# The first feed-forward product by Strassen's scheme, with weight sums made by adding DMAs, in a two-layer encoder on one core

## The chip, the cores and the metric

The kernel runs on one NeuronCore of a Trainium2 chip. TensorE (PE) multiplies, VectorE (DVE) and ScalarE (ACT) work element by element, GpSimd (POOL) and SyncE (SP) issue DMAs here. The metric is the device time of one execution in microseconds, as the median of several runs.

## What is computed

Two layers on x of 512 tokens by 1024 channels, in float32: an attention part with three groups of heads, an output projection, and a feed-forward part of width 4096. The change lies in the feed-forward part, and in small places of the attention.

```python
for i in range(DEPTH):                       # DEPTH = 2
    h = rmsnorm(x, norm_mix[i])
    qa, ka, va, qb, kb, vb, cq, ckv, kr = jnp.split(h @ w_in[i], split_at, axis=-1)
    ...                                      # 6 + 4 + 6 heads, QK norms, rotary keys, biases
    x = x + mixed @ w_out[i]                 # 1024 x 1024
    h = rmsnorm(x, norm_mlp[i])
    x = x + jnp.square(jax.nn.relu(h @ w_up[i])) @ w_down[i]   # 1024 x 4096, 4096 x 1024
```

## The kernel before

**Numbers.** Each float32 operand is split in a high part (`whi`, or the first of a pair of tiles) that PE's fast float32r format holds exactly, and the rest (`wlo`, or the second). `split` does it with a copy, on ACT or DVE, and a subtraction on DVE that reads the source again. `mm3` multiplies two such pairs with three matmuls: high by high, high by low, low by high. Weights come by DMA into `raw` (2 buffers, `wload`) and are split by `wsplit` into `whi` and `wlo` (4 buffers each, 1024 columns).

**Order.** Nothing is issued as the code is written. The class `Plan` records each operation with its tiles, then `schedule` goes through them with assumed costs and delays and places, at each step, the operation that can start first; among equals the one with the lower turn. A turn is the place in the code plus an offset from the table `TURNS`, one offset for eight operations. Buffers of a tag are given out in the order of the code, except for the PSUM banks. A copy that may run on ACT or DVE (`copy`) goes where it would end first. The result is one fixed order for each engine.

**Stages of a layer.** `mix` holds input projections, 16 heads (`attend`, for each head two halves of 256 queries; each half's output sums up in a bank of its own, and `pv_out` adds the two half sums of products that stand in the upper and lower 64 rows), and the output projection in three groups. When the last group of the output projection has ended for half of the channels, `norm_in` transposes x for the channel tiles k, scales and splits them: `xg2[k]`, 512 tokens wide.

**Feed-forward, `mlp`.** The 4096 hidden channels are taken in 4 chunks (`CH`) of 1024. In a chunk, 8 blocks f of 128 hidden channels are made: `w_up` for the block (512 KB) is loaded and split, 8 k times `mm3` with 512 tokens as columns go into one bank, ACT does relu out of the bank, DVE multiplies it with the bank's relu into `sp` (tag `p`). Two blocks that are added and subtracted by Strassen's second product share one `sp`: DVE forms the signed sums (`q0`, `q2`, `q13`), and the hidden pieces A11, A22, A12 and S1 to S4 are split into tiles of the tags tm12, tm9, ma, vb, tm6, o. The second product, `w_down`, goes by Strassen's scheme in Winograd's form: 7 products of half size instead of 8, x_ij with tokens in halves and output channels in halves. Its four weight quarters are loaded whole in 1 MB DMAs into the tag `qk`, and `total` makes four sums of weights on DVE (b1, b2, b3, and b2 again) into the tag `pt`, which `product` splits. `add` adds a finished bank, times the row scale, to x.

The lines read `L326` in the profile of the kernel before, since `emit` issues every operation from one line; so the rows are told apart by tile names.

## Time and profile before

| | us |
|---|---|
| median of 3 runs | 1211.63 (1210.93 to 1211.81) |
| profiled execution, device time | 1210.97 |
| its span, first to last instruction | 1209.0 |
| PE busy in the span | 1194.9 (99%) |
| DVE busy | 1008.5 (83%) |
| ACT busy | 638.9 (53%) |
| POOL busy | 3.5 |
| DMA, share of 16 engines | about a third, 123.9 MB moved |

An engine is busy while it works on an instruction; waiting for a semaphore isn't busy. Matmuls are pipelined, so their rows overlap: the distance between the starts of two is what one costs, not its own duration. Groups of instructions give the tiles written and read, the shape, the count, the busy time, the mean duration, and the idle time of the engine just before.

### The profile page before, as it was taken

How to read it: one execution, taken by the hardware profiler on the slowest of the kernel's cores; microseconds unless marked ns; L12 is line 12 of the kernel's file. 1: busy time of each engine (PE TensorE's matmuls, PEld its weight loads, DVE VectorE, ACT ScalarE, POOL GpSimd, SP SyncE). 2: the span in 40 equal slices, each digit the busy share in tenths (PEclk: the TensorE clock that was granted, in tenths of full speed). 3: DMA queues.
4: the chain of work that ended last, by engine and by line, in shares of the span. 5: the costliest groups of instructions: out<-in, count | busy, mean ns of one | idle time of the engine just before them, and what ended most of it. 6: DMA issues, size and time to landing. Idle time of an engine off the chain costs nothing.

```text
span 1209.0 us, 17753 instructions
## 1 busy us (share of the span) xinstructions
PE 1194.9 (99%) x6624; PEld 1028.3 (85%) x6624; DVE 1008.5 (83%) x1902; ACT 638.9 (53%) x1237; POOL 3.5 (0%) x10
## 2 busy tenths in 40 slices
PE   9999999999999999999999999999999999999998
PEld 8998998788888888888899999887888888888886
DVE  7898899996886887948958988899978869679586
ACT  6667789644423533425547576976643334343242
POOL 1000000000000000000000000000000000000000
PEclk9999999999999999999999999999999999999999
DMA  6221254542133142221142303356322431423301
GB/s 215 95 88 36 75 140 124 165 157 91 67 132 112 70 147 98 75 99 55 60 144 90 106 18 90 105 159 189 117 93 82 139 105 70 138 72 106 104 2 68
DMA packets 36357, 123.89 MB, mean 102 GB/s; under 512 B 4700, under 2 KB 5852, under 8 KB 32176
## 3 DMA queue, kind: packets, MB, share of 16 engines
q1 hardware_dynamic: 36048, 122.41, 31.6%
q8 instruction: 52, 0.85, 0.3%
q0 software_dynamic: 224, 0.36, 0.1%
q14 instruction: 33, 0.27, 0.1%
HBM read 108.29 MB, written 4.24 MB: 93 GB/s over the span
## 4 chain that ended last, share of the span: by engine, by line
PE 89%; ACT 4%; DVE 3%; DMA 1%; issue 1%; SPq 0%; ACTq 0%; DVEq 0%
PE bank L326 89%; ACT p L326 1%; ACT pt L326 1%; DMA qk<-qk 1%; ACT sq L326 0%; DMA v<-in_xT_dram 0%; DVE v L326 0%; ACT pvt L326 0%; DVE pt L326 0%; DVE qk L326 0%; DMA raw<-in_w_out_dram 0%; DVE o L326 0%; DVE p L326 0%; ACT tm L326 0%; DVE tm L326 0%
## 5 line engine op out<-in xcount | busy, mean ns | idle before, releaser
L326 PE MATMUL bank<-fm,whi 128*128 128x512 f32 x1024 | 315.0, 390 | 0.0
L326 PE MATMUL bank<-whi,fm 128*128 128x256 f32 (+2 forms) x1280 | 289.9, 311 | 1.7 <-ACT fm L326 0.8
L326 PEld LDWEIGHTS bank<-fm,whi 128*128 128x128 f32 x1024 | 192.1, 188 | 40.3
L326 PEld LDWEIGHTS bank<-whi,fm 128*128 128x128 f32 x1280 | 211.7, 190 | 13.6 <-ACT whi L326 1.0
L326 PE MATMUL bank<-wlo,fm 128*128 128x256 f32 (+2 forms) x640 | 196.4, 310 | 0.0
L326 PE MATMUL bank<-fm,wlo 128*128 128x512 f32 x512 | 196.3, 390 | 0.0
L326 ACT ACTIVATE whi<-raw 128x1024 fp32r<-128x1024 f32 (+2 forms) x102 | 105.0, 1032 | 168.5 <-PE bank L326 125.0
L326 DVE TENSOR_TENSOR wlo<-raw,whi 128x1024 fp32r<-128x1024 f32 (+2 forms) x122 | 142.2, 1170 | 60.1 <-ACT whi L326 59.5
L326 PE MATMUL bank<-whi,tm 128*128 128x512 f32 x544 | 178.4, 391 | 0.0
L326 PEld LDWEIGHTS bank<-wlo,fm 128*128 128x128 f32 x640 | 121.2, 190 | 5.3 <-DVE wlo L326 0.2
L326 ACT ACTIVATE whi<-pt 128x1024 fp32r<-128x1024 f32 x61 | 64.4, 1061 | 113.4 <-PE bank L326 80.3
L326 PEld LDWEIGHTS bank<-whi,tm 128*128 128x128 f32 x544 | 102.1, 188 | 22.4
L326 PE MATMUL bank<-wlo,tm 128*128 128x512 f32 x304 | 118.1, 391 | 0.0
L326 PEld LDWEIGHTS bank<-fm,wlo 128*128 128x128 f32 x512 | 96.1, 188 | 20.2
L326 PE MATMUL bank<-qk 96*128 96x512 f32 (+3 forms) x304 | 89.1, 395 | 1.4 <-DMA qk<-qk 0.5
L326 DVE TENSOR_TENSOR pt<-bank,pt 128x512 fp32r<-128x512 f32 (+2 forms) x128 | 79.5, 634 | 5.4 <-ACT pt L326 4.3
L326 DVE TENSOR_TENSOR wlo<-pt,whi 128x1024 fp32r<-128x1024 f32 x64 | 77.6, 1218 | 5.8 <-ACT whi L326 5.6
L326 ACT ACTIVATE whi<-qk 128x1024 fp32r<-128x1024 f32 x45 | 47.5, 1059 | 59.8 <-PE bank L326 59.8
L326 PE MATMUL bank<-con_sb,p 128*128 128x128 f32 x464 | 72.9, 275 | 2.8 <-DVE nm L326 1.0
L326 DVE TENSOR_TENSOR wlo<-qk,whi 128x1024 fp32r<-128x1024 f32 x48 | 58.3, 1219 | 19.4 <-ACT whi L326 19.4
L326 ACT ACTIVATE pt<-bank 128x512 fp32r<-128x512 f32 (+2 forms) x125 | 67.0, 552 | 2.3 <-PE bank L326 1.4
L326 PEld LDWEIGHTS bank<-wlo,tm 128*128 128x128 f32 x304 | 57.1, 188 | 12.7 <-DVE wlo L326 0.2
(186 smaller groups left out, 1887.0 us busy)
## 6 DMA issues: line engine op xcount, KB each, us to landing
qk<-in_w_down_dram SPq DMA_DIRECT2D x32, 1024.0 KB, 4.6
raw<-in_w_up_dram SPq DMA_DIRECT2D x64, 512.0 KB, 3.3
raw<-in_w_in_dram SPq DMA_DIRECT2D x28, 512.0 KB, 3.4
qk<-qk SPq DMA_DIRECT2D x78, 128.0 KB, 2.4
raw<-in_w_out_dram SPq DMA_DIRECT2D x16, 512.0 KB, 4.0
ma<-brow SPq DMA_DIRECT2D x12, 448.0 KB, 3.9
raw<-in_w_in_dram SPq DMA_DIRECT2D x8, 288.0 KB, 4.0
v<-in_xT_dram SPq DMA_DIRECT2D x6, 256.0 KB, 5.8
```

Source lines behind the costliest of these rows:

```text
L326: getattr(getattr(nc, o.eng), o.name)(*[real(a) for a in o.args], **{k: real(v) for k, v in o.kw.items()})
```

## The change

**First product.** h @ w_up also goes by Strassen's scheme. `seven` replaces `norm_in`: for two pairs of channel tiles at a time it brings x^T into one tile, splits A11, A22, A12 as they are and, after `combine` has formed the signed sums on DVE, S1 to S4. These tiles lie in the tags fm, qk and pt and stay for the whole layer. In a chunk the 1024 hidden channels are made in two pieces, `piece(0)` and `piece(1)`, each with 7 products of 2 x 4 `mm3` of 256 columns. The two run interleaved in the order of `UP`. The products that are summed share a bank; ACT takes intermediate sums out of the banks, DVE adds.

**Weight sums.** A weight tile `ta` (tag `qk`, two halves of 512 KB) is loaded with w11 and, after it has been split and used, `gps.dma_start(..., accum_op=OP.add)` adds w12, then w22, then w21 to it from DRAM: three versions follow the first, for the first product per piece, for the second product per half. The sum of w12 and w22 alone is made on DVE (in `raw`), since both are needed.

**Relu squared.** ACT does relu and then the square, from SBUF or from the bank, into `sp` (now tag `pt`, two hidden blocks side by side); `combine` forms the signed sums.

**Smaller.** A head's two halves sum up in the two halves of one bank, and `pv_out` runs once per head on 512 columns. `raw` has 3 buffers. The rotary tables lie in a tile `ma`. The running sum of squares (`Stat`) shares the tag `pvt`. `TURNS` is a new table. For adding DMAs `schedule` assumes another delay. `w_up` is laid out in the order in which the pieces read it.

```diff
--- before.py
+++ after.py
...
+UP = "00101100010111"
...
-            lat = self.LAT[e]
+            lat = 2500.0 + o.args[0].size() * 2.5 if e == "gpsimd" and o.name == "dma_start" else self.LAT[e]
...
+    def combine(v):
+        lead = (slice(None),) * (len(v.a.shape) - 1)
+        q0, q1, q2, q3 = (v[lead + (slice(i * 256, (i + 1) * 256),)] for i in range(4))
+        dve.tensor_tensor(q0, q1, q0, OP.subtract)
+        dve.scalar_tensor_tensor(q2, q0, -1.0, q2, OP.mult, OP.subtract)
+        dve.scalar_tensor_tensor(q1, q2, -1.0, q1, OP.mult, OP.subtract)
+        dve.scalar_tensor_tensor(q3, q2, -1.0, q3, OP.mult, OP.subtract)
+    def seven(supply, l, ks):
+        shared = supply(), supply()
+        raws, out = [], []
+        for n, k in enumerate(ks):
+            raw = T([128, 1024], F32, "p", 2)
+            for u in range(2):
+                pt = bank()
+                kk = k + 2 * u
+                for b in range(NB):
+                    pe.transpose(pt[:, b * 128:(b + 1) * 128], x_t[b][:, kk * 128:(kk + 1) * 128], ident)
+                copy(raw[:, u * 512:(u + 1) * 512], pt[:], P(l, G2 + kk))
+            r, sa, sb = ((supply(), supply()) for _ in range(3))
+            split(r[0], r[1], raw[:, 256:768])
+            half = slice(n * 256, (n + 1) * 256)
+            split(shared[0][:, half], shared[1][:, half], raw[:, 768:1024])
+            raws.append((raw, sa, sb))
+            lo, hi = slice(0, 256), slice(256, 512)
+            out.append({"a11": at(r, lo), "a22": at(r, hi), "a12": at(shared, half),
+                        "s3": at(sa, lo), "s1": at(sa, hi), "s2": at(sb, lo), "s4": at(sb, hi)})
+        for raw, sa, sb in raws:
+            combine(raw)
+            split(sa[0], sa[1], raw[:, 0:512])
+            split(sb[0], sb[1], raw[:, 512:1024])
+        return out
...
-        def pv_out(o, e, ps, cols):
+        def pv_out(o, e, ps):
             main, oth = slice(64 * e, 64 * e + 64), slice(64 - 64 * e, 128 - 64 * e)
-            n = cols.stop - cols.start
-            t = T([128, 256], F32, "pvt", 1)
-            copy(t[main, :n], ps[oth, :n])
-            dve.tensor_tensor(o[main, cols], ps[main, :n], t[main, :n], OP.add)
+            t = T([128, S], F32, "pvt", 1)
+            copy(t[main], ps[oth])
+            dve.tensor_tensor(o[main], ps[main], t[main], OP.add)
...
-                    xg2 += [norm_in(k, P(l, G2 + k)) for k in range(4 * h, 4 * h + 4)]
+                    xg2 += seven(lambda: next(supply), l, (4 * h, 4 * h + 1))
...
-            quarter = []
-            for q in range(4):
-                t = T([128, 2048], F32, "qk", QK)
-                dma.dma_start(t[:], w_down[l, :, (c * 4 + q) * 2048:(c * 4 + q + 1) * 2048])
-                quarter.append(t)
-            w11, w12, w21, w22 = quarter
+            def load(t, w):
+                for i in range(2):
+                    dma.dma_start(t[i], w[i])
+            def grow(t, w):
+                for i in range(2):
+                    gps.dma_start(t[i], w[i], accum_op=OP.add)
+            def pair(w, v, use, use2):
+                for i in range(2):
+                    a, b = (T([128, 1024], F32, "raw", 3) for _ in range(2))
+                    dma.dma_start(a[:], w[i])
+                    dma.dma_start(b[:], v[i])
+                    dve.tensor_tensor(a[:], a[:], b[:], OP.add)
+                    use(i, wsplit(a[:]))
+                    use2(i, wsplit(b[:]))
+            def blocks(w, o):
+                return [[w[l, :, o + q * 2048 + i * 1024:o + q * 2048 + (i + 1) * 1024] for i in range(2)] for q in range(4)]
+            w11, w12, w21, w22 = blocks(w_up, c * 8192)
...
-            for j in range(4):
-                sp = T([128, 1024], F32, "p", 2)
-                for u in range(2):
-                    f = c * 8 + u * 4 + j
-                    w = wload(w_up[l, :, f * 1024:(f + 1) * 1024])
-                    ps = bank()
-                    for k in range(KT):
-                        mm3(ps[:], at(w, slice(k * 128, k * 128 + 128)), (xg2[k][0][:], xg2[k][1][:]), k == 0, k == KT - 1)
-                    t = T([128, S], F32, "sq", 2)
-                    act.activation(t[:], ps[:], AF.Relu)
-                    dve.scalar_tensor_tensor(sp[:, u * 512:(u + 1) * 512], ps[:], 0.0, t[:], OP.max, OP.mult)
-                hr, lr, hs, ls = hid[j]
-                split(hr, lr, sp[:, 256:1024])
-                q0, q1, q2 = sp[:, 0:256], sp[:, 256:512], sp[:, 512:768]
-                q13 = sp[:].rearrange("p (x n) -> p x n", n=512)[:, :, 256:512]
-                dve.tensor_tensor(q0, q1, q0, OP.subtract)
-                dve.scalar_tensor_tensor(q2, q0, -1.0, q2, OP.mult, OP.subtract)
-                dve.scalar_tensor_tensor(q13, q2.unsqueeze(1).to_broadcast([128, 2, 256]), -1.0, q13, OP.mult, OP.subtract)
-                split(hs, ls, sp[:])
+            ta = chain()
+            load(ta, w11)
+            def square(t, dst, sign=1.0, src=None):
+                act.activation(t, t if src is None else src, AF.Relu, scale=sign)
+                act.activation(dst, t.rearrange("p (x n) -> p x n", x=2), AF.Square)
+            def piece(i):
+                def times(ps, key, hl, start):
+                    for n in range(2):
+                        for j in range(4):
+                            k = (n * 4 + j) * 128
+                            mm3(ps[:, n * 256:(n + 1) * 256], at(hl, slice(k, k + 128)), xg2[j][key],
+                                start and n == 0 and j == 0, n == 1 and j == 3)
+                w, more = ta[i], lambda v: gps.dma_start(ta[i], v[i], accum_op=OP.add)
+                px = bank()
+                times(px, "a11", wsplit(w), True)
+                e1 = T([128, S], F32, "sq", 2)
+                act.activation(e1[:], px[:], AF.Copy)
+                more(w12)
+                yield
+                py = bank()
+                times(py, "a12", wload(w21[i]), True)
+                dve.tensor_tensor(e1[:], py[:], e1[:], OP.add)
+                sp = T([128, 2, 1024], F32, "pt", 2)
+                square(e1[:], sp[:, :, 256:512])
+                yield
+                pz = bank()
+                times(pz, "s1", wsplit(w), True)
+                e2 = T([128, 1024], F32, "p", 2)
+                z, u = e2[:, :512], e2[:, 512:]
+                act.activation(z, pz[:], AF.Copy)
+                more(w22)
+                yield
+                times(px, "s2", wsplit(w), False)
+                act.activation(u, px[:], AF.Copy)
+                more(w21)
+                yield
+                r12, r22 = (T([128, 1024], F32, "raw", 3) for _ in range(2))
+                dma.dma_start(r12[:], w12[i])
+                dma.dma_start(r22[:], w22[i])
+                dve.tensor_tensor(r12[:], r12[:], r22[:], OP.add)
+                times(px, "s3", wsplit(r12[:]), False)
+                dve.tensor_tensor(z, px[:], z, OP.add)
+                square(z, sp[:, :, 512:768], -1.0)
+                yield
+                times(pz, "s4", wsplit(r22[:]), False)
+                dve.tensor_tensor(u, pz[:], u, OP.add)
+                square(u, sp[:, :, 768:1024], -1.0)
+                for n in range(2):
+                    split(hid[2 * i + n][0], hid[2 * i + n][1], sp[:, n, 256:1024])
+                yield
+                times(px, "a22", wsplit(w), False)
+                e4 = T([128, S], F32, "sq", 2)
+                square(e4[:], sp[:, :, 0:256], 1.0, px[:])
+                combine(sp)
+                for n in range(2):
+                    split(hid[2 * i + n][2], hid[2 * i + n][3], sp[:, n])
+                yield
+            both = piece(0), piece(1)
+            for i in UP:
+                next(both[int(i)])
...
+            def into(ps, a, start):
+                def use(i, hl):
                     for j in range(2):
                         for n in range(2):
                             mm3(ps[n][:], at(a[2 * i + j], slice(n * 128, (n + 1) * 128)), at(hl, slice(j * 512, (j + 1) * 512)),
                                 start and i == 0 and j == 0, i == 1 and j == 1)
+                return use
+            def product(ps, a, w, start):
+                for i in range(2):
+                    into(ps, a, start)(i, wsplit(w[i]) if isinstance(w[i], View) else wload(w[i]))
...
+            ta = chain()
+            load(ta, w11)
             ps_x = [bank(), bank()]
-            product(ps_x, a11, w11, True)
+            product(ps_x, a11, ta, True)
+            grow(ta, w12)
             add(ps_x, t1, c1, 1)
             ps_y = [bank(), bank()]
             product(ps_y, a12, w21, True)
             add(ps_y, t1, c1, 1, True)
-            b1 = T([128, 2048], F32, "pt", 2)
-            total(b1, w11, w12)
-            b2 = T([128, 2048], F32, "pt", 2)
-            total(b2, b1, w22)
-            product(ps_x, s2, b2, False)
+            ps_z = [bank(), bank()]
+            product(ps_z, s1, ta, True)
+            grow(ta, w22)
+            add(ps_z, t2, c2, -1)
+            product(ps_x, s2, ta, False)
+            grow(ta, w21)
             add(ps_x, t1, c2, -1)
-            ps_z = [bank(), bank()]
-            product(ps_z, s1, b1, True)
-            add(ps_z, t2, c2, -1)
-            b3 = T([128, 2048], F32, "pt", 2)
-            total(b3, w12, w22)
-            product(ps_x, s3, b3, False)
+            pair(w12, w22, into(ps_x, s3, False), into(ps_z, s4, False))
             add(ps_x, t2, c2, -1, True)
-            product(ps_z, s4, w22, False)
             add(ps_z, t1, c2, -1, True)
             if not last and c == CH - 1:
                 xg += [norm_in(k, P(l + 1, G1 + k)) for k in range(4)]
-            total(b2, b2, w21)
-            product(ps_x, a22, b2, False)
+            product(ps_x, a22, ta, False)
             add(ps_x, t2, c1, 1, True)
...
```

What stands where, before and after, on three engines. Numbers behind names tell buffers apart.

DVE, kernel before, layer 1, up stage of the second chunk: `p` is the hidden block `sp`, `wlo` the low part of a weight tile, `vb` holds hidden pieces.

```order
L326 SCALAR_TENSOR_TENSOR p_4573<-bank_4490,sq_4561 128x512
L326 TENSOR_TENSOR wlo_4580<-raw_4532,whi_4567 128x1024
L326 TENSOR_TENSOR p_4573<-p_4573 128x256
L326 CAST whi_4602<-raw_4576 128x1024
L326 SCALAR_TENSOR_TENSOR p_4573<-bank_4556,sq_4599 128x512
L326 TENSOR_TENSOR wlo_4610<-raw_4576,whi_4602 128x1024
L326 TENSOR_TENSOR vb_4614<-p_4573,vb_4614 128x768
L326 SCALAR_TENSOR_TENSOR p_4573<-p_4573 128x256
L326 SCALAR_TENSOR_TENSOR p_4573<-p_4573 128x2x256
```

DVE, kernel after, layer 1, start of the up stage of the third chunk. `qk_5045` is `ta` of that chunk; its first version is split in the first row (piece 0) and in `wlo_5455` (piece 1), the second versions in `wlo_5492` and `wlo_5540`, the third of piece 0 in `wlo_5579`.

```order
L333 TENSOR_TENSOR wlo_5398<-qk_5045,whi_5391 128x1024
L333 SCALAR_TENSOR_TENSOR v_3078<-bank_5155,r2p_4106,v_3078 128x512
L333 SCALAR_TENSOR_TENSOR v_3078<-bank_5145,r2m_4109,v_3078 128x512
L333 TENSOR_TENSOR wlo_5425<-raw_5298,whi_5413 128x1024
L333 TENSOR_TENSOR wlo_5455<-qk_5045,whi_5442 128x1024
L333 TENSOR_TENSOR sq_5452<-bank_5440,sq_5452 128x512
L333 TENSOR_TENSOR raw_5348<-raw_5348,raw_5438 128x1024
L333 TENSOR_TENSOR wlo_5492<-qk_5045,whi_5478 128x1024
L333 TENSOR_TENSOR wlo_5504<-raw_5339,whi_5497 128x1024
L333 SCALAR_TENSOR_TENSOR v_3078<-bank_5145,r2p_4106,v_3078 128x512
L333 TENSOR_TENSOR wlo_5540<-qk_5045,whi_5529 128x1024
L333 TENSOR_TENSOR wlo_5579<-qk_5045,whi_5568 128x1024
```

It goes on without a gap:

```order
L333 TENSOR_TENSOR wlo_5601<-raw_5348,whi_5587 128x1024
L333 CAST whi_5631<-qk_5045 128x1024
L333 TENSOR_TENSOR wlo_5639<-raw_5438,whi_5624 128x1024
L333 TENSOR_TENSOR wlo_5651<-qk_5045,whi_5631 128x1024
L333 TENSOR_TENSOR raw_5520<-raw_5520,raw_5614 128x1024
L333 TENSOR_TENSOR p_5543<-bank_5402,p_5543 128x512
L333 TENSOR_TENSOR wlo_5695<-qk_5045,whi_5666 128x1024
L333 TENSOR_TENSOR wlo_5711<-raw_5520,whi_5686 128x1024
L333 TENSOR_TENSOR sq_5704<-bank_5508,sq_5704 128x512
L333 CAST whi_5740<-raw_5614 128x1024
L333 TENSOR_TENSOR p_5543<-bank_5506,p_5543 128x512
L333 TENSOR_TENSOR wlo_5755<-raw_5614,whi_5740 128x1024
```

The row after these is `wlo_5768<-qk_5045,whi_5751`, the fourth version of piece 1. Relu-squares out of a bank are gone from DVE; subtractions for versions of `ta`, sums of weights in `raw`, and additions of `p` or `sq` stand in their place.

POOL, kernel before, all its DMAs: constants and the setup of the first layer.

```order
L326 DMA con_sb_67<-in_con_dram 128x272
L326 DMA tm9_148<-in_table_dram 32x10
L326 DMA tm6_165<-in_onehot_dram 32x1024
L326 DMA tm9_185<-in_nlogc_dram 10x1024
L326 DMA pi_199<-in_pos_dram 128x4
L326 DMA brow_308<-tm9_185 10x1024
```

POOL, kernel after, from the last DMA of the setup to the up stage of the fourth chunk of layer 1; the list goes on in the same way through layer 2.

```order
L333 DMA brow_297<-tm9_175 10x1024
L333 DMA qk_3547<-in_w_up_dram 128x1024 x6
L333 DMA qk_3497<-in_w_down_dram 128x1024 x6
L333 DMA qk_4298<-in_w_up_dram 128x1024 x6
L333 DMA qk_4625<-in_w_down_dram 128x1024 x6
L333 DMA qk_5045<-in_w_up_dram 128x1024 x6
L333 DMA qk_5387<-in_w_down_dram 128x1024 x6
L333 DMA qk_5792<-in_w_up_dram 128x1024 x6
```

Every row with x6 is six adding DMAs, one behind the other on this queue: three for each of two halves of `ta`. Each waits for the split of the version before.

PE, kernel before, up stage: `fm` are the parts of x^T, all 512 tokens wide.

```order
L326 MATMUL bank_5698<-fm_3868,whi_5687 128x512
L326 MATMUL bank_5698<-fm_3855,wlo_5695 128x512
L326 MATMUL bank_5698<-fm_3896,whi_5687 128x512
L326 MATMUL bank_5698<-fm_3916,whi_5687 128x512
L326 MATMUL bank_5698<-fm_3896,wlo_5695 128x512
```

PE, kernel after, the same place in a product of the third chunk: halves of `fm`, `qk` and `pt` tiles with the same weights.

```order
L333 MATMUL bank_5440<-fm_3776,whi_5413 128x256
L333 MATMUL bank_5440<-fm_3783,whi_5413 128x256
L333 MATMUL bank_5440<-fm_3776,wlo_5425 128x256
L333 MATMUL bank_5440<-fm_3776,whi_5413 128x256
L333 MATMUL bank_5440<-fm_3783,whi_5413 128x256
L333 MATMUL bank_5440<-fm_3776,wlo_5425 128x256
```

The pattern of three is the same, the width is 256.

## Rows read from the trace of the kernel before

**Rows 1.** The page: span; busy time, share of the span, instructions.

```profile
span 1209.0 us, 17753 instructions
PE 1194.9 (99%) x6624; PEld 1028.3 (85%) x6624; DVE 1008.5 (83%) x1902; ACT 638.9 (53%) x1237; POOL 3.5 (0%) x10
```

**Rows 2.** Windows by stage; columns in the first line.

```profile
core 0: us, PE busy (x) PEld busy (x) DVE busy (x) ACT busy (x) POOL busy (x), PEclk, DMA share, GB/s
45.00:249.00 204.00, 200.65 (x1431) 183.01 (x1432) 190.23 (x520) 152.93 (x378) 0.00 (x0) 1.00 0.37 107
249.00:633.00 384.00, 384.00 (x1805) 320.56 (x1805) 303.72 (x392) 155.60 (x204) 0.00 (x0) 1.00 0.29 98
645.00:848.00 203.00, 200.17 (x1414) 181.89 (x1412) 186.29 (x492) 150.04 (x365) 0.00 (x0) 1.00 0.38 111
848.00:1205.00 357.00, 357.00 (x1596) 293.21 (x1594) 287.35 (x370) 143.06 (x182) 0.00 (x0) 1.00 0.26 90
```

**Rows 3.** Timeline of PE, up product: start, us, operation; eleven starts between.

```profile
299.84 0.39 PE L326 MATMUL bank<-fm,wlo 128*128 128x512 f32 x1
...
302.56 0.39 PE L326 MATMUL bank<-fm,wlo 128*128 128x512 f32 x1
```

**Rows 4.** Timeline of PE, input projection; between the two, eight starts.

```profile
63.10 0.28 PE L326 MATMUL bank<-wlo,fm 128*128 128x256 f32 x1
...
64.18 0.40 PE L326 MATMUL bank<-whi,fm 128*128 128x256 f32 x2
```

**Rows 5.** Groups by form: shapes and count | busy us, mean ns | idle before.

```profile
L326 DVE TENSOR_TENSOR wlo<-raw,whi 128x1024 fp32r<-128x1024 f32 x108 | 131.2, 1220 | 58.1 <-ACT whi L326 57.6
L326 ACT ACTIVATE whi<-raw 128x1024 fp32r<-128x1024 f32 x93 | 98.7, 1064 | 164.5 <-PE bank L326 121.4 <-DMA raw<-in_w_up_dram 27.7 <-DMA raw<-in_w_in_dram 10.0
L326 DVE SCALAR_TENSOR_TENSOR p<-bank,sq 128x512 f32<-128x512 f32 x64 | 43.7, 684 | 1.8 <-ACT sq L326 1.6
L326 DVE TENSOR_TENSOR pt<-pt,qk 128x1024 f32<-128x1024 f32 x32 | 38.6, 1216 | 0.0
L326 ACT ACTIVATE sq<-bank 128x512 f32<-128x512 f32 x64 | 37.0, 582 | 10.5 <-PE bank L326 7.2 <-DVE p L326 3.0
L326 DVE TENSOR_TENSOR o<-bank,pvt 64x256 f32<-64x256 f32 x64 | 26.8, 418 | 5.6 <-ACT pvt L326 4.4
L326 ACT ACTIVATE pvt<-bank 64x256 f32<-64x256 f32 x63 | 23.8, 378 | 21.8 <-PE bank L326 17.6 <-DVE wlo L326 1.6 <-DVE o L326 1.3
L326 DVE SCALAR_TENSOR_TENSOR p<-p 128x512 f32<-128x512 f32 x32 | 22.0, 688 | 0.6
L326 DVE SCALAR_TENSOR_TENSOR fm<-bank,par_sb,fm 128x512 fp32r<-128x512 f32 x24 | 17.0, 745 | 6.1 <-ACT fm L326 6.1
L326 DVE TENSOR_TENSOR p<-p 128x256 f32<-128x256 f32 x32 | 13.5, 423 | 0.8
L326 DVE CAST whi<-raw 128x1024 fp32r<-128x1024 f32 x15 | 10.4, 691 | 14.6 <-PE bank L326 11.7 <-DMA raw<-in_w_up_dram 1.4 <-DMA raw<-in_w_in_dram 1.4
```

**Rows 6.** DMA issues: operation, count, KB each, us to landing.

```profile
qk<-in_w_down_dram SPq DMA_DIRECT2D x32, 1024.0 KB, 4.6
raw<-in_w_up_dram SPq DMA_DIRECT2D x64, 512.0 KB, 3.3
qk<-qk SPq DMA_DIRECT2D x78, 128.0 KB, 2.4
...
con_sb<-in_con_dram POOLq DMA_DIRECT2D x1, 136.0 KB, 3.5
pi<-in_pos_dram POOLq DMA_DIRECT2D x1, 2.0 KB, 6.2
```

**Rows 7.** Timeline of POOL: start, us, operation.

```profile
1.26 0.71 POOL L326 DMA_DIRECT2D con_sb<-in_con_dram  x1 [0.81 <-POOLq L1176]
```

**Rows 8.** Waits: longest of PE and of SP's queue; total us, times, longest.

```profile
PE bank L326 <- ACT sq L326: 1.4, 1, 1.4
...
SPq L326 <- DVE wlo L326: 538.4, 103, 31.9
```

More of the change, by code (lines that the diff above doesn't have):

```diff
@@ L448, in add @@
             if self.i == 0:
-                self.sum = T([128, S], F32, "ssum", 1)
+                self.sum = T([128, S], F32, "pvt", 1)
                 act.activation(self.sum[:], src, AF.Square)
@@ L958, in mix, with tiles512 @@
         xg2 = []
+        def tiles512():
+            for _ in range(12):
+                yield fmt()[:]
+            for _ in range(2):
+                g = T([128, 4, S], F32R, "qk", QK)
+                for i in range(4):
+                    yield g[:, i]
+            g = T([128, 2, NB, 256], F32R, "pt", 2)
+            for i in range(4):
+                yield g[:, i // 2, 2 * (i % 2):2 * (i % 2) + 2, :].rearrange("p b e -> p (b e)")
+            for _ in range(4):
+                yield fmt()[:]
+        supply = tiles512()
         for n, (ts, r) in enumerate((((5, 6, 7), rc), ((0, 1, 2), ra), ((3, 4), rb))):
@@ L996, in mlp, with chain @@
             st1 = Tokens("r1")
+        def chain():
+            t = T([128, 2048], F32, "qk", QK)
+            return [t[:, :1024], t[:, 1024:]]
         t1, t2 = (2, 3), (0, 1)
@@ L1036, in product, with use @@
-            def product(ps, a, w, start):
-                for i in range(2):
-                    hl = wsplit(w[:, i * 1024:(i + 1) * 1024])
+            w11, w12, w21, w22 = blocks(w_down, c * 8192)
+            def into(ps, a, start):
+                def use(i, hl):
                     for j in range(2):
```

87 lines of the change are left out of this document (50 added, 37 removed).

## The prediction

> **What bounds the kernel now.** I read the page's totals first, then busy time by stage, then single rows. The totals put TensorE (PE) at 99% of the span and VectorE (DVE) at 83% [rows 1]; busy is not peak, so the stages must say which limit is real. By stage [rows 2]: from 249 to 633 us and from 848 to 1205 us, layer 1's and layer 2's output projection and feed-forward, PE has no idle time at all, DVE is busy 303.7 of 384 us (79%) and 287.4 of 357 us (80%), ScalarE (ACT) 41% and 40%. In the two attention stretches (45:249, 645:848) PE lacks only 3.4 and 2.8 us, DVE is busy 190.2 of 204 and 186.3 of 203 us. So the feed-forward ends with PE alone, and its matmuls are at their pitch: in one run of the up product 12 matmuls of 512 columns start in 302.56 - 299.84 = 2.72 us, 0.2267 us each, weights loaded in between at no cost [rows 3]. The clock column reads 1.00 of 2.4 GHz. Nothing else is late there: the longest wait of PE in the whole program is 1.4 us, while SP's queue waits 538 us for free buffers [rows 8], so loads stand ready early.
>
> **Part 1, the up product on PE.** Before: per layer 32 blocks x 8 k x 3 = 768 matmuls of 512 columns, 1,536 in all; x 0.2267 = 348.2 us. After, counted in the order: 2,688 of 256 columns (2 layers x 4 chunks x 2 pieces x 7 products x 24). Half the width is not half the time, and the trace has the case: in the input projection nine 256-column matmuls, with the same pattern of three and a new weight tile as often, start in 64.18 - 63.10 = 1.08 us, 0.120 us each [rows 4]. 2,688 x 0.120 = 322.6 us. **The product is worth -25.6 us**, 3.2 us per chunk; by columns alone an eighth of 348 us (43.5) would be saved, the rest is the dearer short matmul. The down product keeps its matmuls. All of it is on the path, since PE has no idle time there.
>
> **Part 2, what DVE and ACT get for it.** DVE, from the counts of both orders and [rows 5]: 48 more subtractions of a split (176 - 128) at 1.22 = +58.5; 64 totals of weights go, 32 sums for the S3 weights stay: -32 x 1.22 = -39.0; 64 relu-squares from a bank at 0.684 go: -43.8; 48 additions of an evacuated product come, at the 0.684 to 0.688 of that width: +32.9; the signed sums of the hidden pieces go from 96 instructions (32 x 0.688 + 64 x 0.42) to 64 of 512 wide: -49 + 44 = -5; the sums and splits on the input side are 64 instructions, 40 of 256 and 24 of 512 columns (0.42 and 0.684), for 16 of 0.745: +21. Sum: +25 us, 12 per layer. DVE stands then at some 316 of 384 - 12.8 = 371 us in layer 1's stretch, 85% instead of 79%. ACT: 47 more copies of 1.06 = +50; 144 evacuations, relus and squares come and 32 go, at 0.582 each: +65; input side some +17: 66 us per layer, 60% of the stretch. On average both fit below PE, so I charge them nothing there; the cover is thin inside the up stage: per piece of 20.2 us of PE DVE has 7 subtractions (8.5), one sum (1.2), 3 additions (2.1), 4 combinations (2.8) and 4 subtractions of hidden pieces (4.4): 19.0 us, 94%. The down product (7 x 24 x 0.2267 = 38.1 us) leaves 8 us of DVE free and takes the overhang. I take +2 us for it, bounds 0 to +16 (2 us per chunk).
>
> **Part 3, the adding DMAs.** 96 new DMAs of 512 KB on GpSimd's queue (POOL), each behind the split that still reads its target. The trace has no adding DMA. From below: a plain 512 KB load lands in 3.3 us. GpSimd's queue costs more: 136 KB in 3.5 us against 2.4 for 128 KB on SP, so 4.4. If the target must be read too, the data counts double: a 1,024 KB load takes 4.6, 1.3 more, so 5.7; the slowest landing on that queue is 6.2 [rows 6]. Nothing of these bounds it from above, so I keep 4.4 to 10 us for the range and take 5.7; POOL's own 0.71 us of issue [rows 7] is inside a landing. Traffic grows by 12 x 0.5 MB per chunk, 50 MB, on 26 to 29% of the DMA engines' time [rows 2]: some 50%.
>
> Who waits: ACT's copy and DVE's subtraction of the next version wait for the landing; behind them in the same queues stand the evacuations that free PE's banks. The order section has the tightest kind of place, 25 DVE rows from wlo_5398 to wlo_5768, with the first half's versions at 5398, 5492, 5579, 5695 and the second's at 5455, 5540, 5651, 5768. Their work is 25.9 us by [rows 5]. A version can start landing + 1.06 us (its copy on ACT) after the end of the one before. With 5.7 the rows wait 5.0 us in sum and take 30.9 us. PE has 305 matmuls of 256 and 16 of 512 between the first uses of the first and last of these versions: 40.2 us. So the chain is hidden with 9 us to spare. Each further us of landing costs three (three versions in a row): 37.8 us at 8, 43.8 at 10; it passes 40.2 at 8.8.
>
> **Part 4, small things.** A head's halves in one bank: 64 additions of 0.418 become 32 of 0.684 and 64 copies of 0.378 become 32 of about 0.59 [rows 5]: -4.9 us of DVE, -4.9 of ACT, in stretches where DVE is busy 92 to 93%; but the sum of squares now shares its buffer with these copies, a bank is held twice as long, and every turn is new. At most PE's 6.2 us of idle time there can come back; I take -2, bounds -6 to +8. At the change from projection to feed-forward the input needs sums before its S products: DVE has 8 more rows of 0.4 to 0.7 after the last transposes, while A11 and A12 products of the first pieces can run (4 x 2.9 us of PE): +2, bounds 0 to +6 for two layers.
>
> **Sum.** -25.6 + 2 - 2 + 2 = -23.6 us. The profiled execution took 1210.97 us, its span 1209.0, so 2.0 us lie outside; the median of three is 1211.63, 0.7 above. Forecast: 1211.6 - 23.6 = **1188 us**; own range 1180 (nothing added, all of attention's idle back) to 1197.
>
> **Rivals.**
> A. DVE becomes the bound in the up stage. For: 94% there, and four or more waits per stage for POOL's data that it didn't have before; subtractions that stand behind a copy already idle 58 us in the kernel before [rows 5]. Against: 15% free over the whole chunk, and 79% before came without one wait of PE. Price: 1 to 2.5 us per chunk, 8 to 20 us of the 25.6: 1196 to 1209. Chance 17%.
> B. The landing is long and PE waits for it: the slower side. Place: the up stage of all 8 chunks. It decides from a landing of 8.8 us, and eats the whole 3.2 us per chunk at 8.8 + 3.2/3 = 9.9 us. At 10.5 us it adds 8 x 3 x 1.7 = 41 us to the forecast, 1229; at 12 us 77, 1265. For: no row of the kernel shows such a DMA, and DVE is at work nearly all the time beside it. Against: every landing here is at 6.2 or below, with room of 2.6. Chance 17%. The Trainium skill, SBUF — State Buffer, "Who interferes with whom", speaks for B: GpSimd writes the descriptors of its DMAs through a port that it shares with VectorE, and is shut out while a VectorE copy of its fast kind runs. The rows bear on it like this: such copies exist (CAST, 0.69 us for 1,024 elements where a subtraction takes 1.22 [rows 5]), but there are 41 of them in the whole new order, as in the old, so by this rule alone a landing grows by 0.7 us at most, seldom, and B isn't reached.
> C. The gain on PE is there, but the new turns cost it in attention: PE idle there from 6 to 25 us. For: DVE at 92% and a shared buffer; against: DVE and ACT have less to do there. About 1205 to 1212. Chance 5%.
> That the change doesn't do what it says would show in the counts; the order already has 1,536 fewer and 2,688 more matmuls.
>
> **How the numbers follow.** Forecast 61%, A 17%, B 17%, C 5%. The range runs from the lower end of the forecast's own range to where B begins to cost more than the product saves: 1180 to 1215; it leaves out most of B and little else. A measurement of this kernel can tell 0.2%, 2.4 us: faster is below 1209.2. Faster: the forecast, A and half of C, 0.80. Same (1209.2 to 1214.1): half of C and B's near end, 0.05. Slower: the rest of B, 0.15.
>
> **What would show it.** Right: 2,688 matmuls of 256 columns at 0.120 us; PE without idle time between the stages named, each feed-forward stretch 11 to 13 us shorter; adding DMAs landing in 4.4 to 7 us; DVE busy about 1,025 us. A: PE waits for DVE's wlo, sq or p while adding DMAs land early. B: whi or wlo waiting for qk from POOL's queue, and PE behind them. C: PE's idle time in the attention stretches. The forecast is wrong if PE waits over 2 us per chunk, whoever releases it.

## The result and the profile after

The changed kernel takes 1218.76 us (median; 1217.77 to 1219.86), the kernel before, on the same chip, 1211.72 us: the ratio is 1.0056, with a 95% interval of 1.0038 to 1.0073. It is **slower by half a per cent, 7 us**, where the prediction said 1188 us and faster; 1218.76 also lies outside its range. The profiled execution took 1219.29 us, its span 1217.5.

First the page's totals, then the windows by stage (columns as in [rows 2]; the stages lie a little later now):

```profile
PE 1177.6 (97%) x7776; PEld 1063.9 (87%) x7776; DVE 1023.6 (84%) x1891; ACT 756.1 (62%) x1392; POOL 86.6 (7%) x106
...
45.00:249.00 204.00, 201.21 (x1445) 184.84 (x1444) 188.86 (x501) 154.39 (x368) 0.00 (x0) 1.00 0.38 106
249.00:633.00 384.00, 367.14 (x2304) 329.03 (x2304) 309.46 (x402) 216.44 (x303) 41.47 (x48) 0.99 0.68 163
845.00:1190.00 345.00, 334.81 (x2123) 299.24 (x2122) 287.95 (x383) 207.34 (x299) 40.45 (x47) 1.00 0.70 167
```

Against [rows 1], PE is busy 17.3 us less and idle 39.9 us in place of 14.1. Against [rows 2], attention is the same to 0.6 us. All the new idle time lies in the feed-forward, where PE had none: 16.9 and 10.2 us in the two stretches. Over a whole stretch neither DVE nor ACT is full (81% and 56% in the first), but the DMA share has gone from 0.29 to 0.68.

The DMA issues (operation, count, KB each, us to landing, as in [rows 6]) and the two large queues (packets, MB, time as a share of 16 engines) of the kernel after:

```profile
raw<-in_w_up_dram SPq DMA_DIRECT2D x48, 512.0 KB, 5.2
qk<-in_w_up_dram POOLq DMA_DIRECT2D x48, 512.0 KB, 6.1
raw<-in_w_down_dram SPq DMA_DIRECT2D x48, 512.0 KB, 4.1
qk<-in_w_down_dram POOLq DMA_DIRECT2D x48, 512.0 KB, 5.5
...
q1 hardware_dynamic: 40656, 122.41, 31.5%
q0 software_dynamic: 14048, 50.69, 25.0%
```

The adding DMAs (POOLq) land in 6.1 and 5.5 us, about the 5.7 that were taken; these are medians, single ones take up to 8.9 us. What wasn't foreseen is the first line: the plain load of w_up into `raw`, 3.3 us before, takes 5.2.

Who makes PE wait (total us, times, longest), to be set against [rows 8], and below it what ACT's copies and DVE's sums in `raw` wait for:

```profile
PE bank L333 <- ACT whi L333: 14.3, 12, 2.2
PE bank L333 <- DVE wlo L333: 7.7, 10, 1.8
...
ACT whi L333 <- DMA raw<-in_w_down_dram: 42.7, 7, 7.4
ACT whi L333 <- DMA qk<-in_w_up_dram: 27.8, 13, 5.3
ACT whi L333 <- DMA qk<-in_w_down_dram: 21.3, 9, 5.7
DVE raw L333 <- DMA raw<-in_w_up_dram: 25.7, 13, 4.7
DVE raw L333 <- DMA raw<-in_w_down_dram: 19.3, 11, 3.1
```

So both kinds of transfer are waited for: versions of `ta` (qk) and plain loads (raw). ACT's 42.7 us alone would not show a loss, since much of it is there, 34.5 us, in the first kernel of the next section, where the loss is gone. One place of the down stage, from the chain of waits (start, us, what) and from the timelines of DVE and PE (the brackets: idle time before, and who ended it):

```profile
318.65 6.66 DMA raw<-in_w_down_dram
...
325.34 1.23 DVE L333 TENSOR_TENSOR raw<-raw 128x1024 f32<-128x1024 f32 x1 [2.06 <-DMA raw<-in_w_down_dram]
326.48 0.55 DVE L333 CAST o<-pt 128x768 fp32r<-128x768 f32 x1
...
327.09 0.50 PE L333 MATMUL bank<-whi,o 128*128 128x512 f32 x1 [1.70 <-DVE o L333]
```

A load into `raw` could be issued only at 318.65, when DVE had freed a buffer, and took 6.66 us. The sum of w12 and w22 waited 2.06 us for it at the head of DVE's queue. The row behind it is the split of a hidden piece (`o`) whose data were there, and for that PE stood still 1.70 us: the engine named, DVE, was held up by a load.

That load landed behind two adding DMAs, issued at 312.24 and 316.65 and still under way when it was issued: they landed at 320.03 and 324.04, the load at 325.31. By the issue and landing times the whole trace looks like this: of the 96 plain loads into `raw` in the two feed-forwards, 33 were issued with no adding DMA under way and landed in 3.3 us (median), as in the kernel before; 63 were issued behind one, took 5.3 us, and every one of the 63 landed after it.

### The profile page after: what moved, and what is told of

Same layout as the page of the kernel before. It is cut to its first block, busy times and chain, and to the rows that moved or that the text cites. A ratio compares the mean times of both kernels' runs of the same rounds, so it can differ in the third digit from the quotient of the medians.

```text
span 1217.5 us, 20599 instructions
## 1 busy us (share of the span) xinstructions
PE 1177.6 (97%) x7776; PEld 1063.9 (87%) x7776; DVE 1023.6 (84%) x1891; ACT 756.1 (62%) x1392; POOL 86.6 (7%) x106
## 3 DMA queue, kind: packets, MB, share of 16 engines
q0 software_dynamic: 14048, 50.69, 25.0%
## 4 chain that ended last, share of the span: by engine, by line
PE 57%; DVE 15%; DMA 13%; issue 7%; ACT 7%; SPq 0%; DVEq 0%; ACTq 0%; POOL 0%; POOLq 0%
PE bank L333 57%; DVE wlo L333 6%; DMA raw<-in_w_down_dram 4%; DMA qk<-in_w_up_dram 4%; DMA qk<-in_w_down_dram 2%; ACT whi L333 2%; DVE pt L333 2%; DMA raw<-in_w_up_dram 2%; DVE v L333 2%; ACT p L333 1%; ACT sq L333 1%; DVE p L333 1%; DVE o L333 1%; DVE tm L333 1%; DMA qk<-qk 1%
## 5 line engine op out<-in xcount | busy, mean ns | idle before, releaser
L333 PE MATMUL bank<-whi,fm 128*128 128x256 f32 (+2 forms) x1280 | 289.0, 312 | 1.4 <-ACT whi L333 1.3
L333 ACT ACTIVATE whi<-qk 128x1024 fp32r<-128x1024 f32 x123 | 130.0, 1058 | 152.9 <-PE bank L333 98.2
L333 PEld LDWEIGHTS bank<-whi,fm 128*128 128x128 f32 x1280 | 209.9, 190 | 11.5 <-ACT whi L333 1.9
L333 PE MATMUL bank<-fm,whi 128*128 128x256 f32 x1024 | 199.0, 286 | 8.7 <-ACT whi L333 7.0
L333 ACT ACTIVATE whi<-raw 128x1024 fp32r<-128x1024 f32 (+2 forms) x135 | 137.6, 1025 | 111.7 <-PE bank L333 51.3
L333 DVE TENSOR_TENSOR wlo<-raw,whi 128x1024 fp32r<-128x1024 f32 (+2 forms) x154 | 180.8, 1179 | 23.4 <-ACT whi L333 19.0
L333 PE MATMUL bank<-wlo,fm 128*128 128x256 f32 (+2 forms) x640 | 196.7, 311 | 0.1
L333 DVE TENSOR_TENSOR wlo<-qk,whi 128x1024 fp32r<-128x1024 f32 x128 | 156.1, 1220 | 40.5 <-ACT whi L333 40.0
L333 PE MATMUL bank<-whi,tm 128*128 128x512 f32 x544 | 181.3, 394 | 8.2 <-ACT whi L333 6.0
L333 PEld LDWEIGHTS bank<-fm,whi 128*128 128x128 f32 x1024 | 160.3, 192 | 13.7 <-ACT whi L333 9.2
L333 PE MATMUL bank<-fm,wlo 128*128 128x256 f32 x512 | 143.5, 287 | 6.7 <-DVE wlo L333 6.7
L333 PEld LDWEIGHTS bank<-whi,tm 128*128 128x128 f32 x544 | 101.5, 188 | 34.5 <-ACT whi L333 9.3
L333 PEld LDWEIGHTS bank<-wlo,fm 128*128 128x128 f32 x640 | 121.2, 190 | 5.9 <-issue 0.9
L333 PE MATMUL bank<-wlo,tm 128*128 128x512 f32 x304 | 119.5, 394 | 1.1 <-DVE wlo L333 1.0
L333 PE MATMUL bank<-qk,whi 128*128 128x256 f32 x512 | 106.5, 287 | 0.3 <-ACT qk L333 0.3
L333 PEld LDWEIGHTS bank<-fm,wlo 128*128 128x128 f32 x512 | 97.1, 192 | 9.3 <-DVE wlo L333 8.9
L333 POOL DMA_DIRECT2D qk<-in_w_up_dram x48 | 41.6, 866 | 812.5 <-DVE wlo L333 456.9
L333 PE MATMUL bank<-qk 96*128 96x512 f32 (+3 forms) x304 | 87.0, 391 | 2.5 <-DMA qk<-qk 0.8
L333 DVE TENSOR_TENSOR pt<-bank,pt 128x512 fp32r<-128x512 f32 (+2 forms) x128 | 79.5, 633 | 4.9 <-ACT pt L333 4.0
L333 PEld LDWEIGHTS bank<-qk,whi 128*128 128x128 f32 x512 | 82.3, 194 | 1.1 <-ACT qk L333 0.8
L333 DVE TENSOR_TENSOR raw<-raw 128x1024 f32<-128x1024 f32 x32 | 39.2, 1224 | 45.1 <-DMA raw<-in_w_up_dram 25.7
L333 ACT ACTIVATE pt<-bank 128x512 fp32r<-128x512 f32 (+2 forms) x127 | 67.8, 552 | 14.0 <-PE bank L333 13.2
```

The lines of the kernel that those rows point to most:

```text
L333: getattr(getattr(nc, o.eng), o.name)(*[real(a) for a in o.args], **{k: real(v) for k, v in o.kw.items()})
```

## The experiments

Three theories were set against each other. **1**: plain loads into `raw` come late, because the adding DMAs take the DMA engines from them. **2**: the chain of split, adding DMA, split is itself too long for PE. **3**: DVE and ACT have too much to do in the up stage (rival A). The first six kernels keep the changed kernel's order on every engine, and alter only what an operation does as it is issued.

### Small adding DMAs

```diff
+                adding = o.eng == "gpsimd" and "accum_op" in kws
+                if adding:
+                    args = [a[:, :64] for a in args]
```

> The changed kernel with the same order on every engine, but each of the 96 adding DMAs adds only the first 64 of its 1,024 columns (32 KB instead of 512 KB), so the weight sums are left incomplete. It takes their traffic (some 47 of 174 MB) and most of their landing time away. Theory 1 (plain loads into raw land late, because the adding DMAs take the DMA engines from them): raw loads of w_up fall from 5.2 to below 4 us, PE's idle time from 39.9 to some 20 us, time about 1200. Theory 2 (the chain split - adding DMA - split is itself too long for PE): the adding DMAs land in 2 to 3 us instead of 6.1 and 5.5, PE's idle time falls as much, time about 1195 to 1200. Theory 3 (DVE and ACT have too much to do in the up stage, rival A of the prediction): time stays above 1212. This run tells 3 from the other two; 1 and 2 are told apart by the run with small raw loads.

Measured: 1188.0 us, ratio to before 0.9799 (0.9778 to 0.9819); 30.8 us less than the changed kernel, and the time that was forecast. Its page's totals and its DMA issues:

```profile
PE 1167.4 (99%) x7776; PEld 1062.3 (90%) x7776; DVE 1024.3 (86%) x1891; ACT 755.6 (64%) x1392; POOL 86.7 (7%) x106
...
raw<-in_w_up_dram SPq DMA_DIRECT2D x48, 512.0 KB, 3.6
qk<-in_w_up_dram POOLq DMA_DIRECT2D x48, 32.0 KB, 2.5
```

DVE and ACT do the same work in the same order, and PE's idle time is 1185.1 - 1167.4 = 17.7 us. Theory 3 falls. So does a cost of writing the DMAs' descriptors: there are as many packets (14,048) and GpSimd is busy as long (86.7 us) as in the changed kernel. The gain is larger than any theory said. The loads into `raw`, untouched, are back at 3.6 us.

### Copies in place of additions

```diff
+                if adding:
+                    del kws["accum_op"]
```

> The changed kernel, same order, but the 96 DMAs on GpSimd's queue copy their 512 KB over the tile instead of adding to it, so the weights of those products are wrong. It keeps count, size, queue and waits, and takes away what the addition costs beyond a copy. If an adding DMA occupies the DMA engines twice as long per byte (in the trace 50.7 MB of queue q0 take 25.0% of 16 engines, 122.4 MB of q1 31.5%), q0 falls to some 13%, the landing from 6.1 to some 4.4 us and raw loads of w_up from 5.2 to some 4 us. Theory 1 and theory 2 both: PE's idle time halves, time about 1205. Theory 3: above 1214.

Measured: 1194.3 us, ratio 0.9852 (0.9828 to 0.9876). Bytes, packets, queue and waits are the same, so **24.5 of the 30.8 us are the price of adding rather than copying**, more than the 14 us that were expected. Issues and queues:

```profile
raw<-in_w_up_dram SPq DMA_DIRECT2D x48, 512.0 KB, 4.1
qk<-in_w_up_dram POOLq DMA_DIRECT2D x48, 512.0 KB, 4.0
...
q0 software_dynamic: 14048, 50.69, 14.3%
```

### Small plain loads, and both

```diff
+                plain = o.eng == "sync" and isinstance(args[0], View) and not args[0].buf.full
+                if plain:
+                    args = [a[:, :64] for a in args]
```

The second kernel has `if plain or adding:`. `full` marks the first three loads of a layer, which fill the three buffers.

> The changed kernel, same order on every engine, adding DMAs whole; but of the 48 plain loads into raw in each layer's feed-forward all except the first three bring only 64 of 1,024 columns (32 KB), into the same three buffers with the same waits, so the rest of those weights is old data (and the sum in raw takes the larger value in place of adding, at the same cost). Theory 1: these loads land in about 2 us instead of 5.2 and 4.1, PE's idle time falls by at least half of the 26 us it has more than before, time about 1200. Theory 2: PE still waits for the chain of adding DMAs; the time stays above 1212. Theory 3: the same, above 1212.

> Both edits together: adding DMAs and the feed-forward's raw loads bring 64 of 1,024 columns each (weights incomplete), same order, same waits. What remains is the order and the work of PE, DVE and ACT. If the loss is all in transfers (theories 1 and 2), PE's idle time falls to about the 14 us of the kernel before and the time to between 1178 (2,688 matmuls at 0.1163 us) and 1190. Theory 3: above 1205, with PE waiting for wlo and whi behind a DVE or an ACT that has no idle time. What is lost at the change from projection to feed-forward (some 4 us per layer) and by the stretches at half clock behind it should stay in either case.

Measured: 1203.9 us (ratio 0.9928, 0.9913 to 0.9943) and 1189.3 us (0.9807, 0.9792 to 0.9822). The first is neither theory's number but between, and its small loads are not all short: those of w_up land in 3.3 us, where about 2 were expected. (The lower bound of the second expectation took 0.1163 us for a matmul of 256 columns; no row shows that, 0.1194 is measured below.) From the issues and the waits, first of the kernel with small plain loads (L349), then of the one with both small (L350):

```profile
raw<-in_w_up_dram SPq DMA_DIRECT2D x42, 32.0 KB, 3.3
ACT whi L349 <- DMA qk<-in_w_up_dram: 15.8, 11, 2.6
DVE raw L349 <- DMA raw<-in_w_up_dram: 11.3, 9, 3.8
DVE raw L349 <- DMA raw<-in_w_down_dram: 8.9, 7, 2.1
...
raw<-in_w_up_dram SPq DMA_DIRECT2D x42, 32.0 KB, 1.8
DVE raw L350 <- DMA raw<-in_w_up_dram: 1.4, 2, 0.8
DVE raw L350 <- DMA raw<-in_w_down_dram: 1.1, 2, 0.8
```

So cutting the plain loads gained 15 us, and the 15 us from there to 1189.3 went only when the adding DMAs were short too. This second part holds the adding DMAs' own landing, still 5.5 us, and also plain loads: DVE's sums still wait 20.2 us for loads, nearly all of 32 KB, and 2.5 us with both small. How it divides no run shows. One place in the kernel with small plain loads, from the timelines of POOL, ACT and PE:

```profile
525.89 1.86 POOL L349 DMA_DIRECT2D qk<-in_w_up_dram  x2 [8.34 <-DVE wlo L349]
...
534.21 1.06 ACT L349 ACTIVATE whi<-qk 128x1024 fp32r<-128x1024 f32 x1 [1.76 <-DMA qk<-in_w_up_dram]
...
535.32 0.74 PE L349 MATMUL bank<-fm,whi 128*128 128x256 f32 x4 [1.20 <-ACT whi L349]
```

Two adding DMAs are issued, each when DVE has ended the split of the tile that it adds to, from 525.89 to 527.75. The first lands 5.5 us after its issue began, the second 7.3 us after its own, and a plain load of 32 KB issued behind them at 527.75 takes 6.6 us. ACT stands idle for 1.76 us until the second has landed, 6.4 us after its issue ended, and PE waits 1.20 us for ACT's copy. With both kinds small nothing is gained over small adding DMAs alone (1188.0): where these don't stand in the way, the plain loads are early enough with three buffers. So **the whole loss has one cause, the adding DMAs**. They cost by late plain loads (theory 1) and by their own chain (theory 2); the two shares stay open, since each cut also shortens the other's landings (the adding DMAs of w_up went from 6.1 to 5.5 us when plain loads were cut).

### Up stage or down stage

```diff
+                if adding and "w_up" in args[1].tensor.name:
+                    args = [a[:, :64] for a in args]
```

The sister kernel has `"w_down"`.

> The changed kernel, same order, with only the 48 adding DMAs of the first product (w_up) cut to 64 of 1,024 columns; those of the second product (w_down) are whole, so the weight sums of w_up are incomplete. The prediction looked for the danger of adding DMAs in the up stage alone, and gave the down stage 8 us of free DVE time per chunk. All 96 cut gained 30.8 us on the changed kernel's 1218.8. If the prediction's place is right, nearly all of that comes here: about 1190, and the sister run with only w_down cut stays near 1216. If both stages wait alike, as the lengths of the stages in the trace suggest (of layer 1's 18.6 us some 10 lie in up stages and 8 in down stages): about 1201 here and 1205 there.

> The sister run: only the 48 adding DMAs of the second product (w_down) cut to 64 of 1,024 columns, those of w_up whole (weight sums of w_down incomplete). If only the up stage is in danger: about 1216. If both wait alike: about 1205. The sum of both runs' gains says whether the stages are independent: two gains that add up to 30.8 us mean that each stage pays for its own transfers.

Measured: 1205.2 us (0.9943, 0.9924 to 0.9962) and 1203.2 us (0.9925, 0.991 to 0.994): gains of 13.6 and 15.5, in sum 29.1 of 30.8. Each stage pays for its own transfers, about half of the loss each; the difference between the two is within the spread of their executions (1201.9 to 1207.6 and 1200.5 to 1204.2).

### The whole change with an order that knows the landings

If landings are the loss, and no engine lacks throughput, an order made for them should keep all the work and win. The planner had assumed 3.6 us from issue to landing for a plain 512 KB load, and 6.06 for an adding one. So for adding DMAs it had the measured median already (6.1 and 5.5), and for plain loads not (5.2 and 4.1 into `raw`). With the measured landings put in, the planner reckoned 30 us more for the old order. A new `TURNS` table was looked for under each set of assumptions.

```diff
-            lat = 2500.0 + o.args[0].size() * 2.5 if e == "gpsimd" and o.name == "dma_start" else self.LAT[e]
+            lat = 2700.0 + o.args[0].size() * 2.5 if e == "gpsimd" and o.name == "dma_start" else self.LAT[e]
+            if e == "sync" and isinstance(o.args[0], View) and getattr(o.args[1], "tensor", None) is not None:
+                if o.args[1].tensor.name in ("in_w_up_dram", "in_w_down_dram"):
+                    lat = 3600.0 if o.args[0].buf.tag == "raw" else 3300.0
```

The three numbers are 3000, 4200, 3600 in the second and third kernel, 3300, 4800, 4200 in the fourth.

> The changed kernel with all its work, and one change: the planner that fixes the order assumes for the feed-forward's plain 512 KB loads the landing that the trace shows (5.2 us into raw, 4.9 us into qk, in place of 3.6 us for each) and 0.2 us more for adding DMAs, and TURNS is a new table that was looked for with these numbers. In the planner's own reckoning the old order takes 30 us more once these landings are put in, the new one none. Theory 1 + 2 (the loss is landings that the order doesn't expect, not a lack of throughput of any engine): PE's idle time falls to between 15 and 25 us, time 1190 to 1203, faster than the kernel before. Rival (the DMA engines lack the throughput for the traffic, so that no order helps): loads land later still where they are asked for earlier, time above 1212.

> The same with landings assumed longer than the trace's median: 5.8 us for loads into raw, 5.2 into qk, 0.5 us more for adding DMAs, and its own table. If the spread of the landings matters (in the changed kernel's trace some loads into raw take 5.8 to 6.7 us), it is faster than the run with the medians, by 2 to 6 us; if not, slower by the 1 us that the planner reckons. Rival as in the run with the medians: above 1212.

> The whole changed kernel with an order looked for further with the long landings assumed (5.8 us for loads into raw, 5.2 into qk, 0.5 us more for adding DMAs): the planner reckons 2.5 us less than for the order of the run before with these landings, which took 1199.1. If what the planner reckons carries over: 1196 to 1198, PE's idle time a little below. If the remaining loss is spread of landings that the assumed numbers don't hold: no better than 1199.

> The same with landings assumed longer again: 6.4 us for loads into raw, 5.8 into qk, 0.8 us more for adding DMAs, and its own table; the planner reckons 3 us more for it than for the sister run. The step from 5.2 to 5.8 us gained 5.7 us against what the planner reckoned. If the loss still left is landings above 5.8 us: 1193 to 1197, below the sister run. If the landings are covered at 5.8: 1199 to 1202, above it.

| landing assumed for loads into raw | time | ratio to before |
|---|---|---|
| 3.6 us (the changed kernel) | 1218.8 | 1.0056 (1.0038 to 1.0073) |
| 5.2 us | 1204.8 | 0.9943 (0.9928 to 0.9957) |
| 5.8 us | 1199.1 | 0.9902 (0.9875 to 0.9928) |
| 5.8 us, looked for longer | 1196.8 | 0.9876 (0.986 to 0.9893) |
| 6.4 us | 1194.3 | 0.9858 (0.9843 to 0.9872) |

The first missed its range by 2 us; the other three came as expected. That landings above 5.8 us were still part of the loss, as the last one was to tell, is not shown: its step of 2.5 us is no larger than the 2.3 us that searching longer gave with the same assumptions. The last kernel, **1.4% faster than the kernel before with the whole work of the change**, by its totals, issues, queue and layer 1's window:

```profile
PE 1169.7 (98%) x7776; PEld 1063.5 (89%) x7776; DVE 1025.5 (86%) x1889; ACT 753.3 (63%) x1394; POOL 88.8 (7%) x106
...
raw<-in_w_up_dram SPq DMA_DIRECT2D x48, 512.0 KB, 4.9
qk<-in_w_up_dram POOLq DMA_DIRECT2D x48, 512.0 KB, 5.9
...
q0 software_dynamic: 14048, 50.69, 25.4%
...
249.00:629.00 380.00, 375.05 (x2395) 339.04 (x2394) 316.28 (x418) 218.98 (x326) 43.38 (x48) 0.99 0.70 166
```

Landings and DMA share are close to those of the changed kernel; PE's idle time is 22.8 us in place of 39.9. The rival, DMA engines that lack the throughput, falls. Part of the step from row to row may be the search's luck, since each order is new in attention too; that the changed kernel's loss came from the adding DMAs rests on the first six kernels, which leave the order alone. That its order did not expect the landings is shown for the plain loads alone. What the order missed of the adding DMAs, whose median it had, stays open; that single ones land later than the 6.06 us assumed, as the 7.3 us above, is one candidate.

## Why the prediction was wrong, point by point

**Part 1, right.** 2,688 matmuls of 256 columns; in the first up stage 124 of them start in 304.14 - 289.34 = 14.80 us, 0.1194 us each, where 0.120 was taken:

```profile
289.34 0.40 PE L333 MATMUL bank<-fm,whi 128*128 128x256 f32 x2
...
304.14 0.28 PE L333 MATMUL bank<-qk,wlo 128*128 128x256 f32 x1
```

That is 348.2 - 320.9 = 27.3 us less work for PE, against 25.6; in the kernel with small adding DMAs PE is busy 1194.9 - 1167.4 = 27.5 us less than before.

**Part 2, right in what it said of DVE.** DVE is busy 1023.6 us, about the 1,025 that were named (its own terms, Part 4's with them, add up to 1,028); ACT 756.1, 10 less than the sum of its terms. Charged was 2 us for a thin cover. With the same work and short transfers the kernel takes 1188 us, so DVE at 94% of the up stage wasn't the bound: rival A was wrong.

**Part 3, where it failed.** The median landing was right, 6.1 and 5.5 us for 5.7. The step that failed is "So the chain is hidden", with its threshold of 8.8 us: the sum charges nothing for the 96 adding DMAs, and with them short the kernel takes 1188.0 instead of 1218.8 us, 30.8 us less. The threshold was worked out from the durations of 25 DVE rows and the landings of the adding DMAs alone. Three things were missing. First, ACT and DVE take rows in order, and waits for other loads stand in the same queues (`raw` at 325.34 above); in the count they cost nothing. Second, it was one place of an up stage, while the down stage was given away with "8 us of DVE free" and lost 15.5 us. Third, work and waits were summed over 40 us, as if PE could run ahead by that much, while split weights have four buffers; this third point is argued, no run isolates it. Also, "every landing here is at 6.2 or below" holds for medians: a single 1 MB load took 8.8 us in the kernel before, and single adding DMAs up to 8.9. With the plain loads cut to 32 KB and adding DMAs landing in 5.5 us, 15 us of the loss were still there, far below the threshold of 8.8. B's threshold and price fall with the count; its direction was right. Of B's port shared by GpSimd and VectorE nothing shows: the small adding DMAs need as many packets and as much of GpSimd's time, and land in 2.5 us.

**Plain loads, a term that wasn't in the sum.** "So loads stand ready early" was read from SP's queue waiting 538 us for buffers [rows 8]. That row can't show it. In the changed kernel (L333) the same wait is longer, 737.7 us, and loads come late; with small adding DMAs (L337) it is 714.5 us, and the loss is gone:

```profile
SPq L333 <- DVE wlo L333: 737.7, 141, 24.4
...
SPq L337 <- DVE wlo L337: 714.5, 138, 24.3
```

A load that waits for its buffer starts only when the buffer is freed, as at 318.65 above, and whatever lengthens its landing then comes out of the time until its use. The ring has three `raw` buffers, and a sum takes two at once. The loads land in 5.2 us (w_up) and 4.1 us (w_down); cut to 32 KB, at 3.3 and 1.8 us, they gave back 15 us.

**Traffic, mis-sized.** Taken was some 50% of the DMA engines' time for 50 MB more; it is 68 and 70%. The bytes were right (50.7 MB); their price per byte was taken as a plain load's, and is 1.78 times a copy's (below). The 5.7 had counted the data twice for the landing, and not for the share.

**Part 4.** Attention: -2 was charged; PE's busy time from 45 to 249 us went from 200.65 to 201.21, and no gain shows. Change from projection to feed-forward: +2 for both layers; the first alone takes 20 - 16.80 = 3.2 us of PE's time, the second 2.5:

```profile
264.00:284.00 20.00, 16.80 (x102) 14.64 (x101) 19.75 (x40) 17.06 (x37) 2.63 (x3) 0.91 0.38 65
849.00:893.00 44.00, 41.50 (x255) 36.33 (x254) 41.54 (x93) 34.78 (x78) 2.59 (x3) 0.96 0.45 119
```

At the first DVE is full (19.75 of 20 us) with the sums and splits of `seven`. It stays in the kernel with both kinds of transfer short:

```profile
264.00:284.00 20.00, 17.13 (x94) 14.95 (x93) 19.73 (x39) 17.23 (x37) 2.63 (x3) 0.84 0.06 6
```

That kernel's idle time of 1188.1 - 1168.2 = 19.9 us is 5.8 above the kernel before: 1211.6 - 27.3 + 5.8 = 1190.1, where 1189.3 was measured.

**The sum as it came out:** 1211.6 - 27.3 + 5.8 + 15 (gone with small plain loads) + 15 (gone only with small adding DMAs) = 1220, against 1218.8. The two 15 are differences of measured times, so the sum tests only the terms before them. That the kernel with small adding DMAs met the forecast of 1188 is in part luck: the gain was 1.7 us larger than reckoned, and attention and the change of stages together cost 5.8 where Parts 2 and 4 had charged 2. PE's visible idle time, 25.8 us more than before, holds most of the loss; a stop shorter than the 0.17 us by which rows of 0.286 us overlap at a pitch of 0.119 doesn't show as idle, and the clock (next section) is not in it. The rule "wrong if PE waits over 2 us per chunk" fits: 25.8 / 8 = 3.2.

## What to carry to other kernels

When a change adds transfers, price the transfers that are already there again: here a plain load behind an adding DMA landed 2 us later, and what waited for it stalled everything behind it in an in-order queue. Threshold counts over a long stretch hide this; look for the shortest distance between a buffer's release and the use of its next content, in every stage. A queue that waits for free buffers doesn't say that loads are early. And an order that was tuned for a landing is worth making anew when the landing changes: here that decided between 0.6% slower and 1.4% faster with the same work.

## What the runs showed of the hardware

**An adding DMA occupies the DMA engines much longer than a copy.** The same 50.69 MB in the same 14,048 packets took 25.0% of 1217.5 = 304 us as additions and 14.3% of 1193.3 = 171 us as copies, 1.78 times; the landing was 6.1 and 5.5 us against 4.0. GpSimd's own time for 106 DMAs was 86.6 us against 54.9; that alone didn't matter, since the small additions keep 86.7 us. The Trainium skill, Collectives: The Full Stack, "The bandwidth ceiling: the fold count and why AG ≠ RS ≠ AR", explains for the additions of a ReduceScatter that each needs two source reads where a copy needs one, and that it gets half of AllGather's throughput. The trace agrees in kind, with 1.78 in place of 2; that the reason is the same for these DMAs no run shows.

**Neighbours pay.** Plain 512 KB loads of w_up took 3.3 us in the kernel before, 5.2 beside adding DMAs, 4.1 beside copies of the same size, 3.6 beside small additions. A load issued behind an adding DMA didn't overtake it in any of 63 cases in the changed kernel, nor in any of 58 with small plain loads, though most of these bring only 32 KB.

**The clock can fall after a stop.** Three stretches of 10 us show a mean granted clock of 0.83, so a part of each ran at the lower of the two levels, 1.2 GHz instead of 2.4. In each PE had just been idle, for 1.33 us until 277.54, 2.23 until 543.43 and 1.99 until 882.51; the kernel before has such a level only at its end:

```profile
273.00:283.00 10.00, 6.96 (x38) 6.06 (x39) 9.86 (x21) 8.06 (x17) 1.73 (x2) 0.83 0.35 56
540.00:550.00 10.00, 7.77 (x53) 7.56 (x51) 3.74 (x4) 4.20 (x6) 1.72 (x2) 0.83 0.87 169
880.00:890.00 10.00, 8.01 (x52) 7.56 (x52) 10.00 (x19) 9.01 (x17) 1.72 (x2) 0.83 0.47 99
```

By these figures each costs at most 0.17 of 10 us, 1.7 us, and the three 5 us, on top of the stops themselves (an estimate). Not every stop brings it: after one of 1.77 us until 532.59 the clock stayed at 1.00, and the profiled execution with small plain loads has no such stretch with 29.6 us of idle time. Two of the three lie at the change from projection to feed-forward, where the kernel with small adding DMAs has such stretches too (0.83 from 860 to 870 us), so they explain little of the loss.
